# Latent attention, one head at a time, rewritten as pairs of heads with 64-row score products and a written-out order

## The chip, the core and the metric

The kernel runs on one NeuronCore of a Trainium2 chip. The metric is the device time of one execution in microseconds, as a median of several executions. Four engines do the arithmetic: TensorE (PE, matrix products; its weight loads are listed apart as PEld), VectorE (DVE), ScalarE (ACT) and GpSimd (POOL). SyncE (SP) issues most DMA transfers. Each engine works through its own instructions in order and waits on semaphores for the others. On-chip data lie in SBUF (128 partitions); matrix products are written to PSUM, eight banks of 512 float32 per partition.

## The reference

The program is two layers of a trunk over 1024 tokens of width 1024. Layer 0 uses differential attention, layer 1 latent attention; after each comes a gated MLP with a causal convolution of width 3. The change touches the latent attention alone:

```
proj = h @ w_in
c_q  = rms_norm(proj[..., :384], q_norm_g)
c_kv = rms_norm(proj[..., 384:640], kv_norm_g)
k_pe = apply_rope(proj[..., 640:], cos, sin)          # 32 wide, one for all heads
q  = (c_q @ w_uq).reshape(b, s, 16, 64 + 32)          # q_nope, q_pe (rotated)
kv = (c_kv @ w_ukv).reshape(b, s, 16, 64 + 64)        # k_nope, v
sc = (einsum(q_nope, k_nope) + einsum(q_pe, k_pe)) * 96 ** -0.5
p  = softmax(where(k // 64 <= q // 64, sc, min))      # causal in chunks of 64
o  = einsum(p, v).reshape(b, s, 1024) @ w_o
```

Sixteen heads; a query sees the keys of its own and all earlier chunks of 64.

## The kernel before

**Numbers in two parts.** To reach float32 accuracy with a fast product, every operand x is split into a high part (x rounded to the fast type) and a low part (x minus the high part). A product is three passes (`mm3`, L120 to L122): high by low, high by high, low by high. `hi` (L126, L128) makes the high part, on ScalarE unless another engine is named; `lo` (L131) makes the low part, on VectorE unless named.

**PSUM.** Three kinds of tiles share the eight banks: two "S" tiles of 128 x 1024 (two banks each), three "b" banks, one "u" bank.

**The stage.** `mla_input` works token tile by token tile (128 tokens, eight of them). It projects to the latents, normalizes them, transposes them, and makes the values, which go through DRAM (`v_d`) and come back head pair by head pair. Then come 64 steps, one for each head h and each p from 0 to 3. A step covers 256 queries, as two rows of 128 (j = 0, 1; row i = 2p + j has 128(i + 1) keys). Its parts are

- scores: one head's query tile holds 64 plain and 32 rotary rows, and 32 more so that the rotation becomes part of the product (128 rows in all); the key tile holds the matching 128 rows. Three full passes write an S tile in blocks of at most 512 keys. VectorE overwrites the masked corner (L2017), takes the row maximum (L2018); ScalarE takes the exponential with the row sum (L2019);
- VectorE inverts the sum (L2025), GpSimd scales the row (L150);
- PE transposes the weights in 128 x 128 blocks to a "b" bank (L264), ScalarE and VectorE split them (L128, L131);
- PE multiplies with the values, 64 high and 64 low columns side by side, in two passes (L2039, L2040) to the "u" bank; L2042 and L2043 add the halves; ScalarE issues the store of the result to `o_d` (L2045).

Beside the steps run the projections of the next head pair: for each head two halves of 512 tokens of the query (three latent blocks, nine passes each), and for each pair two halves of the keys (two blocks, six passes each). VectorE multiplies the query projection by the rotary table (L1720), ScalarE and mostly GpSimd split it; keys are split head by head in tiles of 64 rows.

**What sets the order.** In this stage the order of each engine's instructions is what the framework's scheduler makes of the program (`steps`, L293 on). In the differential attention of layer 0 it is written out by hand: a table with a line for each step names the parts in the order in which all four engines take them, and `manual_schedule` holds the scheduler to it. That attention's score products (L1884) are of 64 rows: the two halves of the array hold two different products, issued in turns.

After the attention comes the output projection, whose first half reads heads 0 to 7 alone, and the second MLP.

Of the kernel before, what the change touches and what calls it, by code (L numbers as in the profile page):

```python
# [44 lines left out]
class Ring:  # L45
# [5 lines left out]
    def __call__(self, shape, dt=F32):  # L51
        place = self.places[self.n % len(self.places)]
        self.n += 1
        return self.k.at(place, shape, dt)


class Trunk:
# [235 lines left out]
    def steps(self, attend, units, prepare, n, apart=False):  # L293


        steps = []
        for t in range(n + 2):
            now = before = None
            u = []
            if t < n:  # L300
                now = attend(t)
                steps.append(now)
                prepare(t)
                u = units(t)
                now.scores(0)
            if 0 < t <= n:
                before = steps[t - 1]
            alone = u[:-1] if apart else []
            if alone:
                u = u[-1:]  # L310
            self.run(alone or u, 2 if alone else 1)
            if before:
                before.turn()
            self.run(alone)
            if now:
                now.weigh(0)
                now.scores(1)
            self.run(u)
            if before:
                before.product()  # L320
            if now:
                now.weigh(1)
            if t >= 2:
                steps[t - 2].finish()
            yield

# [1213 lines left out]
    def mla_input(self, W, hts, turns, v_d, heads_of):  # L1540
# [24 lines left out]
        kp = [self.at(f"h{4 + half}", [MLA_ROPE, 512]) for half in range(2)]  # L1565
# [3 lines left out]
        def latents(i):  # L1569
# [5 lines left out]
            nat = nats([P, 672])  # L1575
# [4 lines left out]
            nc.scalar.copy(nat[:, 640:672], acc[:, 768:800])  # L1580
            return nat

        def turn(i, nat):
# [11 lines left out]
            for j in range(2):  # L1595
                nc.tensor.transpose(ps[:, j * P : (j + 1) * P], nat[:, (3 + j) * P : (4 + j) * P], self.ident)
            nc.tensor.transpose(ps[:MLA_ROPE, 256:384], nat[:, 640:672], self.ident)
# [3 lines left out]
            nc.scalar.copy(kp[half][:, s], ps[:MLA_ROPE, 256:384])  # L1601

        def values(i):
            half = i // 4
            s = slice((i % 4) * P, (i % 4 + 1) * P)
            vs = self.raw([P, D])
            for b, y in ((0, self.bank("u")), (512, self.bank())):
# [5 lines left out]
                nc.scalar.copy(vs[:, b : b + 512], y)  # L1613
            nc.sync.dma_start(v_d[:, :, i].rearrange("h p e -> p h e"), vs.rearrange("p (h e) -> p h e", e=P))

        def fetch_tab(half):
            late.tab = [self.at(place, [MLA_ROPE, 512]) for place in ("h12", "h13")]
            for x in range(2):
                nc.sync.dma_start(late.tab[x], a["rope_k"][:, x, half * 512 : (half + 1) * 512])

        def rotary(half):
            r = self.rope(rope, kp[half], *late.tab, MLA_ROPE // 2, MLA_ROPE)
            t = nats([MLA_ROPE, 2, 512], F32R)
            self.hi(t[:, 0, :], r[:MLA_ROPE])
            self.lo(t[:, 1, :], r[:MLA_ROPE], t[:, 0, :], nc.gpsimd)
            heads.rotary(half, t)
# [3 lines left out]
        for i in range(NT + 2):  # L1630
            if readies:
                readies.pop(0)()
            if i == NT - 2:
                heads.share(1, 0)
                heads.first(0, 2)
            if i == NT - 1:
                heads.first(4)
# [10 lines left out]
            if i == 4:  # L1648
                fetch_tab(0)
# [4 lines left out]
            if i == 5:  # L1654
                rotary(0)
                fetch_tab(1)
            if i == NT:
                rotary(1)
                heads.share(1, 1)
            if i >= 8:  # L1660
                heads.early()
        return heads

    SHARES = "SSSVVS"
    SHARED_AT = (3, 4, 10, 6)
    ROTARY = "SV"
    VALUES = "SSVSSSSS"
    WEIGHTS = "SVSSSSSS"
    QUERIES = "SSSVSSSSSSSSSSSSSSSSSSSSSSSSSSSS"
    QUERIES_LOW = "VPPVPPVPPPPPPPPPPPPPPPPPPPPPPPPP"  # L1670
# [665 lines left out]
```

## Time and profile before

| | |
|---|---|
| time, median of 3 runs | 2372.34 us (2372.22 to 2372.76) |
| the profiled execution | 2372.74 us, its span 2370.9 us |
| granted TensorE clock | 0.999 |
| PE busy | 2345.3 us, 99% of the span |
| PEld / DVE / ACT / POOL busy | 83% / 81% / 53% / 25% |
| differential attention | about 40 to 480 us |
| latents and values of layer 1 | about 1213 to 1300 us |
| steps of the latent attention | about 1290 to 1650 us |

Rows of the trace give the start of an instruction, how long it lasted, its engine, its line, what it writes and reads, and the shape. A PE pass lasts longer than the distance to the next pass's start, because passes overlap in the array; the distance from start to start is what a pass costs in a stream, and "busy" time overstates how well PE is used.

### The profile page before, as it was taken

The numbers are of one execution on the slowest core, as the hardware profiler recorded it, in microseconds if no ns is written. First come the engines' busy times: TensorE is split into PE (matmuls) and PEld (weight loads), VectorE is DVE, ScalarE is ACT, GpSimd is POOL, SyncE is SP. The second block draws the span as 40 slices with busy tenths as digits, with TensorE's granted clock in tenths as the row PEclk, the third lists the DMA queues.
The fourth block names the chain that finished last, engine by engine and source line by source line (L and its number), as shares of the span: only waits on it lengthen the run. The fifth ranks groups of instructions, "written<-read, shape, count | busy, mean of one in ns | idle before, by whom it ended". The sixth has DMA issues, their size and how long they took to land.

```text
span 2370.9 us, 32976 instructions
## 1 busy us (share of the span) xinstructions
PE 2345.3 (99%) x12146; PEld 1976.2 (83%) x12146; DVE 1919.9 (81%) x3170; ACT 1259.6 (53%) x2315; POOL 583.5 (25%) x465
## 2 busy tenths in 40 slices
PE   9999999999999999999999999999999999999998
PEld 7888888788888888888898889988888888888886
DVE  6777878858888888999865888886588888889997
ACT  5666666745444444354444777775454444443444
POOL 4545444323000000000133666673420000000001
PEclk9999999999999999999999999999999999999999
DMA  3111111332222222652221211133322222227502
GB/s 148 40 36 36 49 37 54 111 134 94 89 80 81 80 89 80 234 174 86 84 99 56 72 33 39 41 98 110 114 79 88 80 80 83 87 80 284 178 1 80
DMA packets 95667, 213.42 MB, mean 90 GB/s; under 512 B 8713, under 2 KB 33937, under 8 KB 95505
## 3 DMA queue, kind: packets, MB, share of 16 engines
q1 hardware_dynamic: 86304, 183.51, 23.5%
q10 hardware_dynamic: 9200, 27.80, 3.2%
q8 instruction: 96, 1.57, 0.3%
q14 instruction: 67, 0.54, 0.1%
HBM read 158.85 MB, written 52.43 MB: 89 GB/s over the span
## 4 chain that ended last, share of the span: by engine, by line
PE 91%; DVE 5%; DMA 1%; ACT 1%; issue 1%; POOL 0%; POOLq 0%; DVEq 0%; SPq 0%; ACTq 0%
PE S L122 14%; PE S L120 14%; PE S L121 14%; PE b L120 9%; PE b L122 8%; PE b L121 8%; PE u L120 5%; PE u L122 5%; PE u L121 4%; PE S L1884 3%; PE b L264 2%; PE u L2040 1%; PE b L1930 1%; PE u L2039 1%; DVE s L131 1%
## 5 line engine op out<-in xcount | busy, mean ns | idle before, releaser
L168 POOL TENSOR_TENSOR st<-st,mhalf 128x1 f32<-128x1 f32 x56 | 35.3, 632 | 1296.1 <-DVE st L165 1287.4
L120 PE MATMUL S<-s,u 128*128 128x512 f32 (+1 forms) x800 | 301.8, 377 | 0.2 <-ACT u L1110 0.2
L122 PE MATMUL S<-s,u 128*128 128x512 f32 (+1 forms) x800 | 301.2, 376 | 0.1
L121 PE MATMUL S<-s,u 128*128 128x512 f32 (+1 forms) x800 | 301.0, 376 | 0.0
L128 ACT CAST u<-h 128x512 fp32r<-128x512 f32 (+1 forms) x194 | 115.8, 619 | 267.1 <-DVE h L1031 262.8
L120 PE MATMUL b<-s,u 128*128 128x512 f32 x588 | 230.8, 393 | 1.1 <-DVE u L131 0.4
L122 PE MATMUL b<-s,u 128*128 128x512 f32 x588 | 229.1, 390 | 0.0
L121 PE MATMUL b<-s,u 128*128 128x512 f32 x588 | 229.0, 389 | 0.0
L1088 DVE SCALAR_TENSOR_TENSOR u<-u,conv,u 128x1023 f32<-128x1023 f32 (+1 forms) x176 | 225.1, 1279 | 0.8 <-ACT u L1084 0.7
L150 POOL TENSOR_TENSOR u<-u,st 128x512 f32<-128x512 f32 (+7 forms) x160 | 173.1, 1090 | 161.1 <-DVE st L2025 107.3
L128 ACT CAST s<-u 128x512 fp32r<-128x512 f32 (+3 forms) x229 | 144.2, 663 | 100.2 <-PE u L122 28.7
L128 ACT CAST u<-b 128x512 fp32r<-128x512 f32 (+1 forms) x256 | 134.9, 547 | 92.1 <-PE b L1930 57.7
L131 DVE TENSOR_TENSOR u<-b,u 128x512 fp32r<-128x512 f32 (+1 forms) x256 | 158.6, 631 | 23.9 <-ACT u L128 22.8
L120 PEld LDWEIGHTS S<-s,u 128*128 128x128 f32 x800 | 150.6, 188 | 27.9 <-ACT u L1110 0.5
L122 PEld LDWEIGHTS S<-s,u 128*128 128x128 f32 x800 | 150.6, 188 | 27.8 <-DVE u L131 0.3
L121 PEld LDWEIGHTS S<-s,u 128*128 128x128 f32 x800 | 150.6, 188 | 27.4
L120 PE MATMUL u<-s,s 128*128 128x512 f32 (+1 forms) x408 | 165.1, 405 | 1.1 <-DVE s L131 0.9
L122 PE MATMUL u<-s,s 128*128 128x512 f32 (+1 forms) x408 | 158.3, 388 | 0.0
L121 PE MATMUL u<-s,s 128*128 128x512 f32 (+1 forms) x408 | 157.6, 386 | 0.0
L131 DVE TENSOR_TENSOR s<-u,s 128x512 fp32r<-128x512 f32 (+2 forms) x205 | 140.8, 721 | 15.0 <-ACT s L128 14.7
L1091 ACT ACTIVATE u<-u 128x1024 f32<-128x1024 f32 x44 | 46.7, 1062 | 187.4 <-DVE u L1088 187.4
L131 DVE TENSOR_TENSOR u<-h,u 128x512 fp32r<-128x512 f32 x171 | 118.1, 691 | 32.4 <-ACT u L128 31.5
(294 smaller groups left out, 6389.6 us busy)
## 6 DMA issues: line engine op xcount, KB each, us to landing
u<-in_ffn_up SPq DMA_DIRECT2D x88, 512.0 KB, 3.9
g_d<-u ACTq DMA_DIRECT2D x44, 512.0 KB, 2.6
u<-in_ffn_down SPq DMA_DIRECT2D x66, 256.0 KB, 4.7
u<-g_d SPq DMA_DIRECT2D x62, 256.0 KB, 4.1
s<-in_da_wqkv SPq DMA_DIRECT2D x23, 512.0 KB, 3.3
x_d<-u SPq DMA_DIRECT2D x16, 512.0 KB, 2.6
s<-x_d SPq DMA_DIRECT2D x8, 1024.0 KB, 10.5
s<-g_d SPq DMA_DIRECT2D x18, 256.0 KB, 5.3
```

What stands on the lines that cost most here:

```text
L120: mm(out, lh, rl, start=first, stop=False, skip_group_check=onto)
L121: mm(out, lh, rh, start=False, stop=False, skip_group_check=onto)
L122: mm(out, ll, rh, start=False, stop=last, skip_group_check=onto)
L128: self.nc.scalar.copy(out, src)
L131: (eng or self.nc.vector).tensor_sub(out, src, hi.bitcast(F32))
L150: self.nc.gpsimd.tensor_mul(x, x, s.to_broadcast(list(x.shape)))
L168: nc.gpsimd.tensor_tensor(r, s, self.mhalf, ALU.pow)
L264: self.nc.tensor.transpose(ps[:, j * P : (j + 1) * P], probs[t][:, k : k + P], self.ident)
L1088: nc.vector.scalar_tensor_tensor(t[half][:, back:], u[half][:, : S - back], w, t[half][:, back:], ALU.mult, ALU.add)
L1091: nc.scalar.activation(t[0], t[0], AF.Silu)
L1884: nc.tensor.matmul(sc[c][:, b : b + m], q[rows, qp, qs], kt[rows, kp, :m], start=x == 0, stop=x == 2)
L1930: k.nc.tensor.transpose(ps[:, j * P : (j + 1) * P], self.e[t][0][:, c : c + P], k.ident)
```

## The change

**Heads in pairs.** A step is now one head pair and 256 queries: 32 steps. The 64 plain query rows of the two heads lie in one tile (head 0 in partitions 0 to 63, head 1 in 64 to 127), the keys likewise. Scores are products of 64 rows, the two heads' in turns (`scores` of the new `MlaStep`, L2080): five terms. Three are the plain part (low by high, high by low, high by high). Two are the rotary part: a tile `r` holds for each head 32 rows of the high and 32 of the low part of the rotated query, and the shared rotary key lies four times in partitions, so that `r` by the key's low and `r` by the key's high part make the rotary part.

**Shared query tiles.** The rotary queries of two head pairs (four heads x 32 rows) are projected together, every second pair (`r_parts`), and rotated with a shuffle, two products and a sum; the 64 plain rows of a pair are projected without the doubled rotary rows. Query scaling moves into the split (`q_parts`, L1745 for the low part).

**Mask as a product.** The corner is no longer overwritten: a sixth pair of 64-row products (L2083) adds a large negative number to it, out of a constant tile and 64 columns of ones.

**Where scores lie.** For p < 2 the two heads' scores share an S tile and one maximum instruction; for p > 1 each head has an S tile of its own, so that one row of scores takes both tiles.

**Values.** They are split before they go to DRAM and are read back ready (twice the bytes); the step that split them after reading is gone. The results' stores are now issued by SP, one in each step, out of two tiles in place of four.

**Order.** `mla_steps` reads a table of 32 lines; each names the parts (S scores, M maximum, E exponential, I inversion, C scaling, T transposes, H and L their split, A products with values, O and P the sum of halves; K, Q, R, W, V, O with numbers: projections and loads; a prime for each step back) in the order in which PE, DVE, ACT and POOL take them. The first four blocks of the output weights are split inside this order.

The PE queue before, in the middle of the stage, around the scores of one head (S tiles; b<-ident are transposes, u the products with values). Two rows of scores, each in three full passes for each block of keys, stand between transposes of the step before:

```order
L2040 MATMUL u_14576<-u_2552_14558,s_2412_13948 128x128
L264 MATMUL b_14617<-ident,u_2544_14520 128x128 x4
L264 MATMUL b_14625<-ident,u_2544_14520 128x128 x3
L120 MATMUL S_14713<-s_1919_11652,s_2434_14039 128x512
L121 MATMUL S_14713<-s_1919_11652,s_2434_14039 128x512
L122 MATMUL S_14713<-s_1919_11652,s_2434_14039 128x512
L120 MATMUL S_14713<-s_1919_11652,s_2434_14039 128x128
L121 MATMUL S_14713<-s_1919_11652,s_2434_14039 128x128
L122 MATMUL S_14713<-s_1919_11652,s_2434_14039 128x128
L120 MATMUL S_14769<-s_1919_11652,s_2434_14039 128x512
```

The PE queue of the change in the eleventh line of the table (p = 0, first row):

```order
L2146 MATMUL u_11986<-u_2187_13237,s_1967_11991 128x256
L2147 MATMUL u_11986<-u_2187_13237,s_1967_11991 128x256
L2080 MATMUL S_13287<-s_2086_12656,s_2087_12660 128x128 x4
L2080 MATMUL S_13287<-s_1917_11652,s_2051_12445 128x128 x4
L2080 MATMUL S_13287<-s_2086_12656,s_2087_12660 128x128 x2
L2083 MATMUL S_13287<-ones,h_1964_11982 128x64 x2
L2118 MATMUL b_13302<-ident,u_2161_13075 128x128
L2118 MATMUL b_13302<-ident,u_2166_13098 128x128 x2
L2146 MATMUL u_11986<-u_2193_13258,s_1967_11991 128x256
```

What moved: five pairs of 64-row passes and a mask pair now serve two heads, and full-height work (values, transposes) stands on both sides of them.

The VectorE queue before, around the same scores: a corner is overwritten (MEMSET) ahead of each maximum.

```order
L131 TENSOR_TENSOR u_2566_14622<-b_14617,u_2566_14622 128x512
L2017 MEMSET S_14713 64x64
L131 TENSOR_TENSOR u_2568_14629<-b_14625,u_2568_14629 128x384
L2018 TENSOR_REDUCE st_2588_14710<-S_14713 128x1
L2017 MEMSET S_14769 64x64
L2018 TENSOR_REDUCE st_2601_14766<-S_14769 128x1
```

The VectorE queue of the change at the end of the tenth line (p = 3, 1024 keys; S_13210 and S_13211 are the two heads') and the start of the eleventh:

```order
L1745 SCALAR_TENSOR_TENSOR s_2188_13241<-b_13175,s_2188_13241 128x512
L2090 TENSOR_REDUCE st_2190_13251<-S_13210 128x1
L2090 TENSOR_REDUCE st_2190_13251<-S_13211 128x1
L131 TENSOR_TENSOR u_2193_13258<-b_13246,u_2193_13258 128x512
L131 TENSOR_TENSOR h_2196_13285<-b_13254,h_2195_13284 128x384
L2090 TENSOR_REDUCE st_2199_13310<-S_13287 128x2
L2107 RECIPROCAL st_2191_13252<-st_2191_13252 128x2
```

What moved: no memset, two maxima of a wide row back to back, one maximum and one inversion for both heads where the row is short.

The diff, cut to its core:

```diff
+    def mla_steps(self, rows, attend, extra):
         steps = []
+        with self.tc.manual_schedule(engines={E.PE, E.DVE, E.Activation, E.Pool}):
+            for t, row in enumerate(rows):
+                for name in row.split():
+                    if name in extra:
+                        extra.pop(name)()
+                        continue
+                    step = t - name.count("'") + name.count("+")
+                    while len(steps) <= step:
+                        steps.append(attend(len(steps)))
+                    steps[step].parts.pop(name.strip("'+"))()
...
+    MLA = (
...
+        "S0 K30h C1a' Pb'''' H0a'' K30l C1b' L0a'' T1a'' M0a T2a'' H1a'' Q30 H2a'' M0b E0a L1a'' A0a''' E0b L2a'' A0b''' T0b'' Oa''' I0 S1 C0a Ob''' Pa''' H0b'' Pb''' Q30h L0b'' Q30l C0b T1b'' M1a T2b'' H1b'' T0a' A0a'' M1b E1a A1a'' A2a'' A0b'' L1b'' H2b''",
+        "S0 E1b' L2b''' T1a'' A1b''' M0 K31 Oa''' I1' C1a' H0a'' Pa''' H1a'' L0a'' S1 E0a L1a'' Q31 K31h M1 C1b' E0b K31l E1a I0 E1b T0b'' C0a Q31h I1",
...
+                vs = self.raw([P, D], F32R)
+                v = vs.rearrange("p (h a e) -> p h a e", a=2, e=64)
+                y = y.rearrange("p (h e) -> p h e", e=64)
+                self.hi(v[:, :, 0, :], y)
+                self.lo(v[:, :, 1, :], y, v[:, :, 0, :])
+                p = b // P
+                nc.sync.dma_start(v_d[p : p + 4, :, i].rearrange("h p e -> p h e"), vs.bitcast(F32).rearrange("p (h e) -> p h e", e=256))
...
+        v_ring, k_ring, q_ring, r_ring = self.ring("s13", "s4"), self.ring("s1", "s12"), self.ring("s11", "s5"), self.ring("s10", "s8")
+        t_ring = self.ring("h10", "h11", "h8")
...
-            P=self.ring("u12", "u6", "u7", "u8", "u9"), pT=self.ring("u0", "u1", "u10", "u11"), o=self.ring("h4", "h5", "h6", "h7"),
+            P=self.ring("u12", "u6", "u7", "u8", "u9", lambda: piece(0), lambda: piece(1)), pT=self.ring("u0", "u1", "u10", "u11", None), o=self.ring("h4", "h5"),
...
+        def project(p, off, n, latent, half):
             acc = self.bank()
+            for k in range(n):
+                wh, wl = (w[:, off + k * P : off + (k + 1) * P] for w in W[p])
+                self.mm3(acc, wh, wl, latent(0, half, k), latent(1, half, k), k == 0, k == n - 1)
+            return acc
+        def q_parts(p, half):
+            s, st = slice(half * 512, (half + 1) * 512), SimpleNamespace()
+            def products():
+                st.acc = project(p, 0, 3, cT.q, half)
+            def high():
+                if half == 0:
+                    pairs[p]["q"] = q_ring([P, 2, S], F32R)
+                nc.scalar.mul(pairs[p]["q"][:, 0, s], st.acc, MLA_SCALE)
+            def low():
+                q = pairs[p]["q"]
+                nc.vector.scalar_tensor_tensor(q[:, 1, s], st.acc, MLA_SCALE, q[:, 0, s].bitcast(F32), ALU.mult, ALU.subtract)
+            return {"": products, "h": high, "l": low}
...
+        def r_parts(p, half):
+            s, st, n = slice(half * 512, (half + 1) * 512), SimpleNamespace(), MLA_ROPE // 2
+            def products():
+                st.acc = project(p, 640, 3, cT.q, half)
+            def swap():
+                st.sw = t_ring([P, 512])
+                nc.vector.stream_shuffle(st.sw, st.acc, [i + n if i < n else i - n for i in range(32)])
+            def cosines():
+                st.r = t_ring([P, 512])
+                nc.vector.tensor_mul(st.r, st.acc, cosine[:, s])
+            def sines():
+                nc.gpsimd.tensor_mul(st.sw, st.sw, sine[half])
+            def add():
+                nc.gpsimd.tensor_add(st.r, st.r, st.sw)
+            def high(x):
+                if half == 0 and x == 0:
+                    t = r_ring([P, 2, S], F32R)
+                    for y in range(2):
+                        pairs[p + y]["r"] = t[:, y, :]
+                self.hi(pairs[p + x]["r"][:, s], st.r)
+            def low(x, c):
+                t = pairs[p + x]["r"][:, s]
+                src, dst = (slice(64 * c + 32 * y, 64 * c + 32 * y + 32) for y in (x, 1 - x))
+                self.lo(t[dst], st.r[src], t[src])
+            out = {"": products, "s": swap, "m": cosines, "p": sines, "a": add, "h": lambda: high(0), "g": lambda: high(1)}
...
+            R.mask = [self.at("h9", [P, P], F32R)]
+            nc.vector.tensor_scalar_mul(R.mask[0], self.ones.bitcast(F32), 0.0)
+            for c in range(2):
+                nc.vector.tensor_scalar_mul(R.mask[0][64 * c : 64 * c + 1, 0:64], self.ones[64 * c : 64 * c + 1, 0:64].bitcast(F32), NEG)
+            R.u = self.bank("u")
...
     def scores(self, j):
+        k, nc, hd = self.k, self.k.nc, self.hd
         i = 2 * self.p + j
         n = (i + 1) * P
+        q, kt, r, key = hd["q"], hd["k"], hd["r"], self.key[0]
         qs = slice(i * P, (i + 1) * P)
+        if self.one:
+            self.both[j] = k.big().rearrange("p (c n) -> p c n", c=2)[:, :, :n]
+            sc = [self.both[j][:, c, :] for c in range(2)]
+        else:
+            sc = [k.big()[:, :n] for _ in range(2)]
+        self.sc[j] = sc
         for b, m in blocks(n):
-            k.mm3(sc[:, b : b + m], q[:, 0, qs], q[:, 1, qs], kt[:, 0, b : b + m], kt[:, 1, b : b + m], True, True)
-        nc.vector.memset(sc[0:64, n - 64 : n], NEG)
+            s = slice(b, b + m)
+            terms = [(q[:, 1, qs], kt[:, 0, s]), (q[:, 0, qs], kt[:, 1, s]), (r[:, qs], key[:, 1, s]), (r[:, qs], key[:, 0, s]), (q[:, 0, qs], kt[:, 0, s])]
+            last = b + m == n
+            for x, (lhs, rhs) in enumerate(terms):
+                for c in range(2):
+                    rows = slice(64 * c, 64 * c + 64)
+                    nc.tensor.matmul(sc[c][:, s], lhs[rows], rhs[rows], start=x == 0, stop=x == 4 and not last, skip_group_check=last)
+        for c in range(2):
+            rows = slice(64 * c, 64 * c + 64)
+            nc.tensor.matmul(sc[c][:, n - 64 : n], self.R.mask[0][rows], k.ones[rows, 0:64], start=False, stop=True, skip_group_check=True)
+    def peak(self, j, c):
+        k = self.k
+        if j not in self.nm:
+            self.nm[j], self.l[j], self.e[j] = k.stat(2), k.stat(2), [None, None]
+        nm = self.nm[j] if c is None else self.nm[j][:, c : c + 1]
+        k.nc.vector.tensor_reduce(nm, self.both[j] if c is None else self.sc[j][c], axis=AX.X, op=ALU.max, negate=True)
+    def exp(self, j, c):
+        k, p = self.k, self.p
+        n = (2 * p + j + 1) * P
+        if p > 1:
+            e = self.R.P([P, S])[:, :n]
+        else:
+            x = j if p else 0
+            if x not in self.tile:
+                self.tile[x] = self.R.P([P, S])
+            off = c * 512 if p else j * 512 + c * 256
+            e = self.tile[x][:, off : off + n]
+        self.e[j][c] = e
+        k.nc.scalar.activation(e, self.sc[j][c], AF.Exp, bias=self.nm[j][:, c : c + 1], accum_out=self.l[j][:, c : c + 1])
...
+    def product(self, g, c):
+        k, nc, p = self.k, self.k.nc, self.p
+        if g == 0:
+            self.o[c] = self.R.u[:, c * 256 : c * 256 + 256]
+        o = self.o[c]
+        for kb, (ah, al), c0 in k.key_blocks(p, {x: self.pt.get((x, c), self.pt[g, c]) for x in range(p + 1)}):
+            if kb // 2 == g:
+                v = self.V[self.pair][:, kb, c].rearrange("p a e -> p (a e)")
+                nc.tensor.matmul(o[:, c0:], v, al, start=kb == 0, stop=False)
+                nc.tensor.matmul(o[:, c0:], v, ah, start=False, stop=kb == 2 * p + 1)
+    def copy(self, c):
+        if self.t is None:
+            self.t = self.R.o([64, 512])
+        self.k.nc.scalar.copy(self.t[:, c * 256 : c * 256 + 256], self.o[c][64:128])
+    def add(self, c):
+        t = self.t[:, c * 256 : c * 256 + 256]
+        self.k.nc.vector.tensor_add(t, t, self.o[c][0:64])
+        if not any(x in self.parts for x in ("Pa", "Pb")):
+            self.k.nc.sync.dma_start(self.dst, self.t.rearrange("e (c s) -> e c s", c=2))
...
```

365 lines of the change are left out of this document (158 added, 207 removed), and 30 rows, old and new, of the table MLA.

## The prediction

> **What bounds the kernel now.** I read first the busy times and the chain of waits on the page, then the busy time by stretches, then the instructions in order of time.
>
> ```profile
> PE 2345.3 (99%) x12146; PEld 1976.2 (83%) x12146; DVE 1919.9 (81%) x3170; ACT 1259.6 (53%) x2315; POOL 583.5 (25%) x465
> PE 91%; DVE 5%; DMA 1%; ACT 1%; issue 1%; POOL 0%; POOLq 0%; DVEq 0%; SPq 0%; ACTq 0%
> ```
>
> PE sets the time, and 91% of the chain is PE. So only two things count: what PE has to issue, and how long it finds nothing ready. In the next view each row is a stretch: its length, then the busy time of PE, PEld, DVE, ACT and POOL (instructions in brackets), the granted clock, the DMA's share and GB/s.
>
> ```profile
> 100.00:400.00 300.00, 300.00 (x1760) 245.21 (x1759) 237.53 (x436) 189.72 (x386) 149.77 (x107) 1.00 0.13 44
> ...
> 1300.00:1320.00 20.00, 17.66 (x95) 14.11 (x93) 18.04 (x33) 15.99 (x29) 14.20 (x10) 1.00 0.31 105
> 1320.00:1560.00 240.00, 239.30 (x1559) 215.50 (x1559) 199.08 (x488) 181.19 (x401) 157.73 (x128) 1.00 0.14 42
> 1560.00:1650.00 90.00, 87.76 (x560) 77.54 (x560) 69.42 (x154) 63.83 (x134) 52.09 (x40) 1.00 0.37 113
> 1290.00:1650.00 360.00, 354.72 (x2258) 315.20 (x2257) 293.65 (x692) 266.60 (x577) 229.34 (x180) 1.00 0.22 67
> ```
>
> In the stage that changes (1290 to 1650), PE is visibly idle for 360 - 354.72 = 5.3 us, 2.3 of them as the steps begin, 2.2 in the end, 0.7 in the 240 us between. The first row is the differential attention, with 64-row scores and a written-out order: no idle time at all in 300 us, with VectorE at 79%, ScalarE at 63%, GpSimd at 50%. It is the nearest thing to the changed stage that this trace has, and I take two prices from it. The clock is 1.00 throughout, so it is no term.
>
> **What a pass costs.** The distance from start to start is the price. Full height, in this stage:
>
> ```profile
> 1377.25 0.40 PE L121 MATMUL S<-s,s 128*128 128x512 f32 x1
> 1377.49 0.39 PE L122 MATMUL S<-s,s 128*128 128x512 f32 x1
> 1377.72 0.22 PE L120 MATMUL S<-s,s 128*128 128x128 f32 x1
> 1377.77 0.28 PE L121 MATMUL S<-s,s 128*128 128x128 f32 x1
> 1377.89 0.27 PE L122 MATMUL S<-s,s 128*128 128x128 f32 x1
> 1378.00 0.44 PE L120 MATMUL S<-s,s 128*128 128x512 f32 x1
> ...
> 1378.74 0.28 PE L120 MATMUL S<-s,s 128*128 128x256 f32 x1
> 1378.86 0.28 PE L121 MATMUL S<-s,s 128*128 128x256 f32 x1
> ```
>
> 512 columns cost 0.23 us, 256 cost 0.12, 128 cost 0.11 (the first one 0.05); 384 I put between, at 0.18. Half height, in the differential attention (x6 is three pairs, x12 six):
>
> ```profile
> 197.59 0.60 PE L585 MATMUL b<-ident,h 128*128 128x128 f32 x4
> 198.12 1.66 PE L1884 MATMUL S<-u,u 64*128 64x512 f32 x12
> 199.70 0.50 PE L120 MATMUL u<-s,s 128*128 128x512 f32 x1
> 200.04 0.40 PE L121 MATMUL u<-s,s 128*128 128x512 f32 x1
> ...
> 222.09 0.39 PE L122 MATMUL u<-s,s 128*128 128x512 f32 x1
> 222.41 0.97 PE L1884 MATMUL S<-u,u 64*128 64x512 f32 x6
> 223.31 0.55 PE L1930 MATMUL b<-ident,u 128*128 128x128 f32 x3
> 223.61 0.48 PE L1975 MATMUL b<-h,ones 128*128 128x512 f32 x1
> 223.93 0.40 PE L1976 MATMUL b<-h,ones 128*128 128x512 f32 x1
> ```
>
> Six pairs take 199.70 - 198.12 = 1.58 us, three take 223.31 - 222.41 = 0.90. So a further pair costs (1.58 - 0.90) / 3 = 0.23: two 64-row passes run at once for the price of one full pass. But 0.90 - 3 x 0.23 = 0.21 comes on top for each group. Also the pass before it is 0.32 long in place of 0.23 (222.09 to 222.41), and the first full pass behind it 0.34 (199.70 to 200.04). An excursion into half height and back to full passes thus costs 0.09 + 0.21 + 0.11 = 0.41. With three transposes behind it, they and the pass after them take 0.30 + 0.32 (223.31 to 223.93). Between full passes the same takes 0.24 + 0.32:
>
> ```profile
> 1440.85 0.49 PE L264 MATMUL b<-ident,u 128*128 128x128 f32 x3
> 1441.09 0.48 PE L120 MATMUL b<-s,u 128*128 128x512 f32 x1
> 1441.41 0.39 PE L121 MATMUL b<-s,u 128*128 128x512 f32 x1
> ```
>
> which is 3 x 0.11 + 0.23, so transposes beside full passes carry no charge. Behind half height they add 0.06, and the excursion makes 0.36. I take 0.38.
>
> The Trainium skill ("TensorEngine Tiling (Array Packing)", section Tiling Modes) says that changing the tiling mode drains TensorE, and its section Overview gives up to 2x for contractions of 64 rows or fewer. The trace agrees with both: the pair at 0.23 is the 2x, the 0.38 are the drains. By the second alone the sum below would lack its fourth term, which is the first rival.
>
> **PE's sum.** Four terms.
>
> Projections: before, 16 heads x 2 halves x 9 query passes and 8 pairs x 2 x 6 key passes, 384; after, 8 x 2 x (9 + 6) and 4 x 2 x 9 rotary ones, 312. 72 x 0.23 = -16.6.
>
> Scores: a head's eight rows have two blocks of 128, two of 256, two of 384, six of 512: one pass over all costs 2 x (0.11 + 0.12 + 0.18) + 6 x 0.23 = 2.20. Before, 16 heads x 3 x 2.20 = 105.6. After, 8 pairs x 5 terms x 2.20 = 88.0. -17.6.
>
> Mask: 64 extra pairs of 64 columns. The nearest row is the 128-column pass: 0.11, or 0.05 for the first one, whose successor's weights are not the limit. Half of 0.05 is the lower bound. 64 x 0.03 to 64 x 0.11 is 1.9 to 7.0; I take 7.0, since 128 columns already cost nearly what 256 do, so narrower passes stop getting cheaper. The Trainium skill ("TensorE: Matmul & The Clock Gate", section LDWEIGHTS) puts a weight load at the columns of the weights over 1.2 GHz whatever the rows; by it a mask pair would be an estimated 0.107 us, 6.8 in all.
>
> Excursions: 64 rows of scores, one for each j of 32 steps. Before, full passes join full passes and transposes without a charge. After, 64 x 0.38 = +24.3. If the mask's weight load falls into the drain, less; the 0.38 was read from three-pair and six-pair groups, which bounds it at 0.36 to 0.42, 23 to 27.
>
> Eight transposes of the latents grow from 32 to 128 columns: below 1 us, +0.6. Transposes (576) and value products (640) stay. Sum: -16.6 - 17.6 + 7.0 + 24.3 + 0.6 = **-2.3 us**. The 34 us that the counts promise are nearly eaten by drains and mask.
>
> **PE's idle time.** The waits behind it:
>
> ```profile
> PE S L120 <- ACT u L2019: 1.8, 3, 1.3
> PE b L264 <- DVE u L131: 1.1, 3, 0.6
> ```
>
> Eight such lines (5.1 us) make 13 waits; these are the longest. Each is longer than it looks by 0.16 us, since a pass lasts 0.39 and its successor is due after 0.23: 5.3 + 13 x 0.16 = 7.4 us, and gaps under 0.16 don't show at all. A written-out order had none in 300 us above, with less loaded helpers. In the new order the first steps lie among the value products, and the end among the output projection of heads 0 to 7, so both ragged places have cover. I take 10 us lost now and 2 then, **-8**; bounds 0 (nothing regained) and -12.
>
> **The other engines,** which only matter if they become late:
>
> ```profile
> L131 DVE TENSOR_TENSOR s<-b,s 64x512 fp32r<-64x512 f32 x30 | 20.6, 686 | 1.3 <-ACT s L128 0.8
> L1720 DVE TENSOR_TENSOR h<-b,u 128x512 f32<-128x512 f32 x30 | 20.6, 685 | 9.8 <-PE b L122 9.2
> L2018 DVE TENSOR_REDUCE st<-S 128x1 f32<-128x1024 f32 x16 | 19.6, 1223 | 1.2
> L2025 DVE RECIPROCAL st<-st 128x1 f32<-128x1 f32 x128 | 19.5, 152 | 7.9 <-ACT u L2019 7.6
> L2017 DVE MEMSET S<- 64x64 f32 x127 | 14.2, 112 | 10.4 <-PE S L122 8.9
> L249 DVE STREAM_SHUFFLE h<-h 32x512 f32<-32x512 f32 x1 | 0.7, 725 | 0.0
> L2019 ACT ACTIVATE u<-S,st 128x1024 f32<-128x1024 f32 x16 | 17.9, 1117 | 6.5 <-DVE st L2018 4.1 <-DVE st L2025 2.0
> L2019 ACT ACTIVATION_READ_ACCUMULATOR u<-S,st 128x1 f32 x128 | 25.3, 198 | 0.0
> L131 POOL TENSOR_TENSOR s<-h,s 128x512 fp32r<-128x512 f32 x28 | 36.2, 1294 | 1.0 <-ACT s L128 0.4
> L131 POOL TENSOR_TENSOR s<-u,s 128x1024 fp32r<-128x1024 f32 x9 | 21.6, 2395 | 2.5 <-ACT s L128 1.9 <-DVE st L2025 0.6
> s<-x_d SPq DMA_DIRECT2D x8, 1024.0 KB, 10.5
> ```
>
> VectorE loses the memsets (14), 32 table products (32 x 0.685 = 22), half the inversions (10), half the key lows (11). It gains 16 query lows (11), eight shuffles and eight products for the rotation (11), and 32 rotary lows of 32 rows. These cost a full 0.69 each, as the 32-row shuffle does (22). -13 in the stage, and 16 value lows of 0.69 (+11) ahead of it, where PE is the limit. So about 281 us of VectorE beside 350 of PE: 80%, what the written-out stage has. GpSimd loses the 36 us of query lows and gains eight pairs of rotary operations. ScalarE loses half its key and query splits. All this is hidden by PE; uncovered, nothing of it would exceed PE's time. The value loads double to 1 MB, at 10.5 us each as the x_d loads, and are issued many steps ahead: hidden. Stores and loads now share SP's queue: a weight load that waits for its buffer holds back a store behind it, and with two result tiles a store late by two steps (20 us) would stop ScalarE's copy and then PE. Since a buffer is freed by one GpSimd low of some 2.4 us, I charge nothing.
>
> **Sum.** The profiled execution took 2372.74, the median is 2372.34, 0.4 less. 2372.34 - 2.3 - 8 = **2362 us**.
>
> **Rivals.**
>
> 1. *The drains cost less* because the mask pair and the next transposes fill them, or the five terms stream better than three. Without the fourth term: 2372.3 - 16.6 - 17.6 + 1.9 + 0.6 - 8 = 2333. For it, the counts; against it, every 64-row group I looked at. 6%; half of the drains gone (2346) is the same case.
> 2. *No idle time comes back:* helpers as loaded as now stall PE as often. 2372.3 - 2.3 = 2370, no change that could be told. For it: VectorE is at 82% and ScalarE at 74% of this stage; in the model stage ScalarE has 63%. 19%.
> 3. *The score tiles become the bound: slower.* A wide row (p > 1, 32 of them) takes both S tiles at once; the next row of scores can start only after maximum and exponential of one or both heads. At 1024 keys: 1.22 + 1.22 for the maxima, then 1.12 + 0.20 for the second exponential, 3.8 us. In the tenth line PE has between its two rows three groups of transposes (1.3), a query projection (9 x 0.23 = 2.1) and two value products (1.0): 4.4. The margin is 0.6 us. If VectorE reaches the first maximum 1.1 us late in each of 32 rows, 0.5 is lost 32 times: 2370 + 16 = 2386. It decides from a mean lateness of 0.9 us on (0.3 x 32 = 10, which uses up the gain). For it: before, a row needed one tile and the other was free. Against: the table alternates wide rows with narrow ones, and hides this in line after line. 10%.
>
> My forecast has 65%. **Range:** the forecast's own 2354 to 2367; for 8 in 10, with the second rival and the near edge of the others, 2350 to 2375. A change of 0.2% (4.7 us) is about what can be told from none. Faster by more: 0.60 of the forecast's 0.65, the first rival, and a little of the second, where a few microseconds return: 0.70. Same: 0.05 and most of the second, 0.18. Slower: the third and some unlucky mixture, 0.12.
>
> **What would show it.** Right: 64-row groups of five pairs at 512 columns that take 5 x 0.23 + 0.11 + 0.2; about 64 of them with a 0.09 longer pass ahead; 312 projection passes; stage length 10 us less; PE idle under 2 us. Wrong: waits of S products on the exponential (third rival), of transposes on the lows (second), or groups without the 0.2 (first). A change in the MLP stages, whose code is the same, would be outside all of this.

## The result: slower by 16 us

The changed kernel takes 2388.77 us (median of 4; 2386.05 to 2389.40) where the kernel before took 2372.53 beside it (2372.22 to 2372.76): a ratio of 1.0066, 95% interval 1.0049 to 1.0084. The forecast was 2362, its range 2350 to 2375. Two single executions among the experiments, of 5191.73 us (experiment 4) and 3866.71 us (experiment 3), lie far above all others of their kernels and count in no time below.

First the busy times of the page, then PE, PEld, DVE, ACT and POOL in stretches of the profiled execution (span 2387.0 us):

```profile
PE 2342.4 (98%) x12586; PEld 1963.2 (82%) x12586; DVE 1912.1 (80%) x2976; ACT 1233.5 (52%) x2290; POOL 560.5 (23%) x447
```

```profile
1290.00:1320.00 30.00, 21.80 (x117) 16.67 (x117) 16.84 (x30) 13.77 (x35) 17.79 (x15) 0.83 0.51 168
1560.00:1660.00 100.00, 91.77 (x699) 79.96 (x696) 63.65 (x111) 63.03 (x141) 53.84 (x42) 0.97 0.26 78
1290.00:1650.00 360.00, 334.96 (x2600) 287.70 (x2598) 268.41 (x467) 234.96 (x541) 201.56 (x159) 0.98 0.21 67
```

Before, PE stood idle for 5.3 us in 1290 to 1650; now for 360 - 334.96 = 25, and the granted clock, which was 1.00 throughout, falls to 0.83 and 0.97 in two places. What PE waited for in this stage (total, times, longest):

```profile
PE S L2080 <- ACT u L2104: 14.4, 5, 8.2
PE u L2146 <- DVE h L2156: 4.7, 9, 0.6
PE b L2118 <- DVE s L131: 3.2, 3, 1.1
PE b L2118 <- DVE st L2107: 1.3, 1, 1.3
```

With four more lines (1.2 us) that makes 24.8 us in 23 waits, in place of 5.1 in 13. Two single waits of score products for exponentials are 13.8 of them. The first, as PE, ScalarE and SP show it:

```profile
1303.24 0.25 PE L2083 MATMUL S<-ones,h 64*128 64x64 f32 x2
1311.69 1.43 PE L2080 MATMUL S<-s,s 64*128 64x256 f32 x10 [8.20 <-ACT u L2104]
1312.92 0.25 PE L2083 MATMUL S<-ones,h 64*128 64x64 f32 x2
1313.11 0.79 PE L120 MATMUL b<-s,u 128*128 128x512 f32 x1
1313.70 0.63 PE L121 MATMUL b<-s,u 128*128 128x512 f32 x1
1314.12 0.63 PE L122 MATMUL b<-s,u 128*128 128x512 f32 x1
```

```profile
1308.13 1.67 ACT L128 CAST u<-u 128x640 fp32r<-128x640 f32 x2 [7.60 <-DMA u<-in_mla_w]
1310.18 0.69 ACT L2104 ACTIVATE u<-S,st 128x512 f32<-128x512 f32 x1
```

```profile
1299.74 2.29 SPq L1600 DMA_DIRECT2D v_d<-u  x2
1302.71 2.87 SPq L136 DMA_DIRECT2D u<-in_mla_w  x2
SPq L136 <- DMA v_d<-u: 2.6, 2, 2.0
```

Read from below: the raw weights of head pairs 1 and 2 are loaded into the same two tiles (`u14`, `u15`) from which the values are stored. So the loads are issued only when the last value stores have left, at 1302.7. The written order has the cast of these weights (`W1h` in the table's first line) ahead of the exponentials `E1a E1b`. ScalarE stands for 7.6 us, the exponentials come 8 us late, and the next row of scores with them. Behind it, 512-column passes come 0.42 apart for some microseconds instead of 0.23: the lower clock.

The second lies at the end, as PE, ScalarE, GpSimd and SP show it:

```profile
1595.96 2.50 PE L2080 MATMUL S<-s,s 64*128 64x512 f32 x10 [5.60 <-ACT u L2104]
1593.99 0.62 ACT L128 CAST h<-u 128x512 fp32r<-128x512 f32 x1 [5.40 <-DMA u<-o_d]
1595.02 0.79 ACT L2104 ACTIVATE u<-S,st 128x640 f32<-128x640 f32 x1
```

```profile
1586.93 4.70 POOL L131 TENSOR_TENSOR s<-u,s 128x1024 fp32r<-128x1024 f32 x2 [1.04 <-ACT s L128]
SPq L646 <- POOL s L131: 5.1, 2, 3.3
```

It is the same pair of tiles. The output projection's first operand load waits until GpSimd has split the output weights that lie there; its cast, which the scheduler put into ScalarE's queue between the lines of the table, stands ahead of an exponential.

### The profile page after: what moved, and what is told of

It is laid out like the page before. It is cut to its first block, busy times and chain, and to the rows that moved or that the text cites. A ratio compares the mean times of both kernels' runs of the same rounds, so it can differ in the third digit from the quotient of the medians.

```text
span 2387.0 us, 33667 instructions
## 1 busy us (share of the span) xinstructions
PE 2342.4 (98%) x12586; PEld 1963.2 (82%) x12586; DVE 1912.1 (80%) x2976; ACT 1233.5 (52%) x2290; POOL 560.5 (23%) x447
## 3 DMA queue, kind: packets, MB, share of 16 engines
q1 hardware_dynamic: 91136, 195.05, 24.8%
## 5 line engine op out<-in xcount | busy, mean ns | idle before, releaser
L128 ACT CAST u<-h 128x512 fp32r<-128x512 f32 x192 | 114.5, 619 | 264.7 <-DVE h L1013 262.6
L120 PE MATMUL b<-s,u 128*128 128x512 f32 x572 | 225.2, 394 | 0.4 <-DVE u L131 0.4
L121 PE MATMUL b<-s,u 128*128 128x512 f32 x572 | 223.3, 390 | 0.0
L122 PE MATMUL b<-s,u 128*128 128x512 f32 x572 | 223.1, 390 | 0.0
L128 ACT CAST u<-b 128x512 fp32r<-128x512 f32 (+1 forms) x232 | 122.6, 549 | 138.0 <-PE b L1965 57.7
L128 ACT CAST s<-u 128x512 fp32r<-128x512 f32 (+2 forms) x221 | 135.5, 650 | 104.5 <-PE u L122 29.6
L150 POOL TENSOR_TENSOR u<-u,st 128x128 f32<-128x128 f32 (+7 forms) x129 | 138.3, 1089 | 143.2 <-DVE st L2107 61.9
L131 DVE TENSOR_TENSOR u<-b,u 128x512 fp32r<-128x512 f32 (+1 forms) x232 | 143.0, 634 | 30.0 <-ACT u L128 29.9
L131 DVE TENSOR_TENSOR s<-u,s 128x512 fp32r<-128x512 f32 (+2 forms) x203 | 138.6, 717 | 15.6 <-ACT s L128 15.3
L131 DVE TENSOR_TENSOR u<-h,u 128x512 fp32r<-128x512 f32 x171 | 118.2, 691 | 32.8 <-ACT u L128 31.7
## 6 DMA issues: line engine op xcount, KB each, us to landing
s<-x_d SPq DMA_DIRECT2D x8, 1024.0 KB, 10.1
```

The lines of the kernel that those rows point to most:

```text
L120: mm(out, lh, rl, start=first, stop=False, skip_group_check=onto)
L121: mm(out, lh, rh, start=False, stop=False, skip_group_check=onto)
L122: mm(out, ll, rh, start=False, stop=last, skip_group_check=onto)
L128: self.nc.scalar.copy(out, src)
L131: (eng or self.nc.vector).tensor_sub(out, src, hi.bitcast(F32))
L150: self.nc.gpsimd.tensor_mul(x, x, s.to_broadcast(list(x.shape)))
```

## The experiments

**1. The two single waits.** Theory A: both come from the shared pair of raw tiles. Theory B: the two score tiles bound the rows (the prediction's third rival), and the loads only happen to be waited for at the same time.

The raw weights of pairs 1 and 2 in tiles that are free at that time:

```diff
-        raw = self.raw([P, w])
+        raw = self.at(place, [P, w]) if place else self.raw([P, w])
...
-            raws[p] = self.fetch(..., 640 if p % 2 else D)
+            raws[p] = self.fetch(..., 640 if p % 2 else D, {1: "u10", 2: "u11"}.get(p))
```

> The changed kernel with one edit: the raw weights of pairs 1 and 2 get tiles of their own (u10, u11) in place of the two tiles that they share with the value stores. Theory A (late loads ahead of hand-ordered work): the 8.2 us in which the score products of the second row wait for ScalarE's exponentials, which stand behind a cast that waits 7.6 us for these weights, goes, and with it the slower passes right after it (granted clock 0.95 in that 100 us): some 2.5 us. Time 2378, and the granted clock of 1300 to 1400 back at 1.00. Theory B (the two score tiles themselves bound the rows, the weights only happen to be waited for at the same time): the wait moves to the next exponential; time 2386 to 2389, and score products still wait for some 8 us in that place.

Measured: 2379.88 us (1.0032 of before, 1.0020 to 1.0045), 8.9 less than the change; 1.9 us less of a gain than expected. SP issues the two loads at 1284.65 and 1290.69, ahead of the last four value stores. The second of them, and the stretch of the first wait:

```profile
1290.69 0.35 SPq L136 DMA_DIRECT2D u<-in_mla_w  x1
1290.00:1320.00 30.00, 29.28 (x182) 22.77 (x181) 23.51 (x40) 19.12 (x46) 21.86 (x18) 1.00 0.52 176
```

PE is busy for 29.28 us in place of 21.80, and the clock is back at 1.00.

The output projection's operand loads in tiles of their own:

```diff
-        X = [None] * NT
+        X, raw = [None] * NT, self.ring("h12", "h13")
...
-                into = self.project(i, range(0, 4), W, o_d, os, self.raw)
+                into = self.project(i, range(0, 4), W, o_d, os, raw)
```

> The changed kernel with one other edit: the output projection's first operand loads get tiles of their own (h12, h13, free since the rotary is done) in place of the shared pair. Theory A: ScalarE's 5.4 us of waiting for such a load, between two exponentials, goes, and with it 5.6 us of idle TensorE and about 2 us of slower passes behind it (granted clock 0.97): 2381. Theory B: the score products wait for the next thing; 2387 to 2389.

Measured: 2383.16 (1.0046; 1.0031 to 1.0061), 5.6 less; 2 us less of a gain than expected.

Both:

> Both edits. Theory A: the two holes are apart (1303 and 1590 us) and add up: 10.7 + 7.6 = 18 us off 2388.8, so 2370.5, which is within 0.2% of the kernel before (2372.5): the change without the holes is worth about nothing, since its TensorE work is 4 us less and the small waits (some 15 us) stay about as many as before. If the order by rows had returned the idle time as forecast, it would be 2362. Theory B: 2384 or more.

Measured: 2374.26 (1.0009; 1.0000 to 1.0018), 14.5 less, the sum of the two. Theory A holds, and B falls: the scores' wait for exponentials shrinks from 14.4 us to 1.5. But what is left lies 3.8 us above the expected 2370.5, and is not the forecast of 2362. In 1290 to 1650:

```profile
1290.00:1650.00 360.00, 347.36 (x2675) 298.03 (x2675) 275.20 (x478) 239.36 (x550) 203.96 (x161) 1.00 0.23 72
PE u L2146 <- DVE h L2156: 4.7, 9, 0.6
PE b L2118 <- DVE s L131: 3.8, 4, 1.1
PE S L2080 <- ACT u L2104: 1.5, 4, 0.9
PE b L2118 <- DVE st L2107: 1.3, 1, 1.3
```

With three short lines, 12.3 us in 22 waits, still 7 more than before. The next experiments start from this kernel.

**2. What the 64-row products cost.** The five terms of a block over all 128 rows, three for one head and two for the other, so that the mode never changes. These are not the reference's scores. One mask pass of 128 rows stays, for the first head alone:

```diff
-                for c in range(2):
-                    rows = slice(64 * c, 64 * c + 64)
-                    nc.tensor.matmul(sc[c][:, s], lhs[rows], rhs[rows], start=x == 0, ...)
+                c = x % 2
+                nc.tensor.matmul(sc[c][:, s], lhs, rhs, start=x < 2, ...)
```

> The kernel with both edits, and its score products without the 64-row mode: each of the five terms of a block goes over all 128 rows in one pass, three of them to the first head's tile and two to the second's, and only the first head's block is masked. The scores are so not the reference's, and the time is that of the same number of columns without a change of mode. If the 64 excursions cost what the sum says (64 x 0.38 us), TensorE's work falls by 24 us, and the time by 15 to 24, since VectorE and ScalarE have 15 to 40 us of slack in that stage: 2347 to 2356. If the drains hide behind the weight loads or are a reading of modelled ends, the time stays at that of the kernel with both edits, 2370.

Measured: 2361.75 (0.9956; 0.9943 to 0.9970), 12.5 less: a gain, but a smaller one than the first case expected. The same place in three kernels, from the last pass before a group of ten pairs to the first transpose behind (the second one too in full rows): both tile edits, then full rows (lines shifted by one), then the kernel of the next experiment, without mask products (lines shifted back by one):

```profile
1392.62 0.27 PE L2118 MATMUL b<-ident,u 128*128 128x128 f32 x1
1392.82 2.58 PE L2080 MATMUL S<-s,s 64*128 64x512 f32 x20
1395.24 0.19 PE L2083 MATMUL S<-ones,h 64*128 64x64 f32 x2
1395.36 0.33 PE L2118 MATMUL b<-ident,s 128*128 128x128 f32 x1
```

```profile
1389.59 0.27 PE L2119 MATMUL b<-ident,u 128*128 128x128 f32 x1
1389.62 2.52 PE L2080 MATMUL S<-s,s 128*128 128x512 f32 x10
1391.97 0.19 PE L2084 MATMUL S<-ones,h 128*128 128x64 f32 x1
1392.00 0.30 PE L2119 MATMUL b<-ident,s 128*128 128x128 f32 x1
1392.14 0.27 PE L2119 MATMUL b<-ident,u 128*128 128x128 f32 x1
```

```profile
1393.58 0.27 PE L2117 MATMUL b<-ident,u 128*128 128x128 f32 x1
1393.78 2.58 PE L2080 MATMUL S<-s,s 64*128 64x512 f32 x20
1396.30 0.33 PE L2117 MATMUL b<-ident,s 128*128 128x128 f32 x1
```

2.74, 2.41 and 2.72 us. The 64-row group thus costs 0.33 more than full rows here (1395.36 - 1392.62 less 1392.00 - 1389.59), its mask pair 0.02. Between a projection and transposes, at 512 columns, it is 0.31 and 0.04. So the drains are real: 64 x 0.32 = 20 us of TensorE work. PE's waits grow as they go, to 17.2 us in 26, so the time falls by less than the work.

The 20 us are not the whole price, because the mask pass that full rows keep isn't free. Here it takes 0.03 itself, and the transpose behind it 0.14 (1392.00 to 1392.14) in place of 0.11; where a value product or a projection follows, that pass takes some 0.08 longer. The mean of 54 such places in this trace is 0.10. The 64-row group with its mask pair costs 0.30 more than full rows in the mean of the 51 rows of scores that no wait disturbs. I estimate from both that an excursion with its mask pair costs about 0.4 us more than full rows without a mask, 64 x 0.4 = 26 us; the sum had 24.3 + 7.0.

**3. The mask.** Filled by VectorE as before the change:

```diff
-            nc.tensor.matmul(sc[c][:, n - 64 : n], self.R.mask[0][rows], k.ones[rows, 0:64], ...)
...
+        k.nc.vector.memset(self.both[j][0:64, :, n - 64 : n] if c is None else self.sc[j][c][0:64, n - 64 : n], NEG)
```

> The kernel with both tile edits and the mask as it was before the change: a fill of 64 rows by VectorE ahead of each maximum in place of the product of 64 columns; in the rows with two short score blocks one fill covers both heads, so 96 fills of about 0.11 us instead of 64 pairs of products. By the prediction's sum the products cost TensorE 7.0 us (64 x 0.11), with bounds of 1.9 to 7.0. If all of this counts, the time falls from 2374.3 to about 2367, less what the fills put on the way from scores to maximum, 64 x 0.11 to 0.2 us, where TensorE waits for it; Rival: the way through maximum and exponential is as tight as TensorE there, and the time stays at 2373 to 2376.

Measured: 2377.06 (1.0020; 1.0012 to 1.0029): 2.8 more than with the products. Not even the rival's range holds it. The profiled execution, of 2375.12, was the shortest of the ten:

```profile
1290.00:1650.00 360.00, 342.61 (x2533) 286.10 (x2532) 287.83 (x567) 239.09 (x547) 203.56 (x161) 1.00 0.22 70
```

VectorE's busy time goes from 275.20 to 287.83 us, and PE's waits from 12.3 to 16.5. Beside 64-row scores a mask as a product is nearly free on TensorE and takes some 12 us off VectorE; this part of the change is worth having.

**4. A low part that waits for GpSimd.** The line `PE b L2118 <- DVE s L131` is in the main three waits of 1.1 us, 85 us apart. VectorE's rows ahead of the first, and GpSimd's:

```profile
1360.66 0.68 DVE L2090 TENSOR_REDUCE st<-S 128x2 f32<-128x512 f32 x1
1361.37 2.22 DVE L131 TENSOR_TENSOR s<-h,s 32x512 fp32r<-32x512 f32 x1
1359.31 3.75 POOL L150 TENSOR_TENSOR u<-u,st 128x1024 f32<-128x1024 f32 x2 [4.19 <-DVE st L2107]
```

A rotary low of 32 rows takes 2.22 us in place of 0.69, and behind three more such lows stands the key low that frees the bank. First, only the order on VectorE (and one place on ScalarE), in three places:

```diff
-... Q21 R21u E1a I0 R21g R21v C0a E1b R21w C0b T0b'' K21h I1",  "S0 R21x C1a' H0b''' K21l C1b' ...
+... Q21 K21h E1a I0 K21l R21u R21g R21v C0a E1b R21w C0b T0b'' I1",  "S0 R21x C1a' H0b''' C1b' ...
```

> The kernel with both tile edits (2374.3 us) and one more edit in the order: in the three places, 85 us apart, where TensorE's transposes wait 1.17 us for a PSUM bank, VectorE takes the low part of the key projection (which frees that bank) ahead of three of the four 32-row rotary lows, and ScalarE its high part one place earlier; nothing else is moved. Theory C (the 32-row lows, 0.69 us each and 2.22 us where one falls behind a GpSimd product, hold up what stands behind them on VectorE, and that ends on TensorE): three times 1.17 us go: 2370.8. Rival D (three banks are too few there, and the wait moves to the next transposes): 2374 to 2375. The 2.22 us low itself is expected to stay in the trace, since the GpSimd product beside it has not moved.

Measured: 2371.37 (0.9996; 0.9987 to 1.0005), 2.9 less: theory C. One part of the expectation missed: the long low is gone as well. Moved behind the key low, it starts at 1362.71, at the end of the GpSimd product, and takes 0.68.

Second, the order as it was, but the scaling beside that low on ScalarE:

```diff
-        self.k.scale(self.e[j][c], self.l[j][:, c : c + 1], "P")
+        self.k.scale(self.e[j][c], self.l[j][:, c : c + 1], "A" if self.pair in (1, 3, 5) and (self.p, j, c) == (3, 1, 1) else "P")
```

> The kernel with both tile edits (2374.3 us, its rotary low of 2.22 us in three places), with one scaling of 128x1024 in each of these three places moved from GpSimd to ScalarE; the order stands. Theory G (a 32-row low, whose operands both lie in SBUF, can't run while a GpSimd product runs, and waits for its end): without that product beside it the low takes 0.69 us, and the transposes behind it wait some 0.2 us instead of 1.17, if ScalarE, which gets 1.05 us more, does not hold them up instead: 2371. Rival H (the low is slow there for another reason, its source or its place in the queue): it stays at 2.2 us, and the time at 2374.

Measured: 2371.14 (0.9995; 0.9986 to 1.0004), 3.1 less.

```profile
1361.45 0.68 DVE L131 TENSOR_TENSOR s<-h,s 32x512 fp32r<-32x512 f32 x1
1359.39 1.90 POOL L150 TENSOR_TENSOR u<-u,st 128x1024 f32<-128x1024 f32 x1 [4.14 <-DVE st L2107]
```

The same low, in the same place of VectorE's queue, without a GpSimd product beside it: 0.68. Theory G. The mean of the lows in the stage falls from 932 to 767 ns:

```profile
L131 DVE TENSOR_TENSOR s<-h,s 32x512 fp32r<-32x512 f32 x28 | 26.1, 932 | 0.9
L131 DVE TENSOR_TENSOR s<-h,s 32x512 fp32r<-32x512 f32 x28 | 21.5, 767 | 0.9
```

**5. The rest of the small waits.** The largest group is `PE u L2146 <- DVE h L2156`. One bank holds both heads' outputs; the program orders every read of it against every product into it, whichever head's columns they touch:

```profile
1371.51 0.27 PE L2147 MATMUL u<-u,s 128*128 128x128 f32 x1
1371.88 0.41 DVE L2156 TENSOR_TENSOR h<-h,u 64x256 f32<-64x256 f32 x1 [0.74 <-ACT u L128]
1372.34 0.39 PE L2146 MATMUL u<-h,s 128*128 128x256 f32 x1 [0.56 <-DVE h L2156]
```

VectorE's sum for one head (its copy is done at 1371.01) starts only when the other head's products have ended, and the next product waits for it. The profile puts VectorE's 0.74 us down to a cast that the sum doesn't read; but in the seven longest of these waits the sum starts 0.03 to 0.10 us behind the end of the other head's last product, so I read that as its releaser. The last kernel starts from the one with the key low first and moves some 95 more entries of the table by a few places, in 24 of its 32 lines; one of them (the ninth) before and after:

```diff
-        "S0 E1b' L2b''' T0a'' M0 T0b'' H3b''' S1 H0b'' I1' L3b''' E0a C1a' L0b'' K30 Oa''' M1 E0b C1b' A0b''' I0 E1a Pa''' A1b''' A2b''' C0a H0a'' A3b''' E1b L0a'' C0b T0a' Ob''' I1",
+        "S0 E1b' L2b''' M0 T0b'' H3b''' S1 H0b'' I1' L3b''' T0a'' Oa''' M1 E0b E0a C1a' C1b' A0b''' I0 E1a Pa''' L0b'' K30 C0a A1b''' A2b''' H0a'' A3b''' E1b L0a'' C0b T0a' Ob''' I1",
```

Between `Pa'''` and the next products (`A1b'''`) a key projection now stands, and covers the sum.

> Both tile edits, the key low first, and further moves in the table of rows: some 110 of its 1455 entries stand a few places earlier or later, none is added or dropped, and what each computes is the same. They go against the waits that the trace of the kernel with the key low first still shows in this stage, each of 0.15 to 1.4 us and most of them three times, 85 us apart: products that wait while ScalarE or VectorE reads the one PSUM bank that both heads' outputs share (5.3 us in 11 places), scores that wait for exponentials (1.5 us), transposes that wait for a bank (2 us). Theory E (these waits are a matter of order alone): with the durations of that trace laid out in the new order, 10 to 12 us of them are gone: 2371.4 falls to 2360, some 0.5% under the kernel before. Rival F (VectorE, ScalarE and GpSimd, each 50 to 80% busy here, pass the delay on, and the waits turn up elsewhere): 2368 to 2372.

Measured: 2361.24 (2359.67 to 2362.05): 0.9952 of before, 0.9938 to 0.9966. Theory E. It takes less time than the kernel before and the change. All of PE's waits in the stage, and the stage's busy times:

```profile
PE u L2146 <- DVE h L2156: 0.9, 3, 0.3
PE b L2118 <- DVE s L131: 0.8, 1, 0.8
PE b L120 <- DVE u L131: 0.4, 1, 0.4
PE S L2080 <- ACT u L2104: 0.2, 1, 0.2
PE b L2118 <- DVE h L131: 0.2, 1, 0.2
1290.00:1650.00 360.00, 356.66 (x2743) 307.37 (x2742) 278.43 (x488) 243.41 (x557) 204.73 (x163) 1.00 0.25 80
```

2.5 us in 7 waits. GpSimd's products still catch rotary lows here, and the longest wait that is left (0.8 us, at 1313) stands behind one of them, of 2.58 us at 1309.79; behind the others TensorE no longer waits for a low.

## Why the prediction was wrong

**The step that failed is PE's idle time:** "I take 10 us lost now and 2 then, -8; bounds 0 (nothing regained) and -12." A loss was excluded, and a loss it was: the listed waits went from 5.1 to 24.8 us. Three things stood behind the step.

1. *The comparison with the differential attention.* I took a written-out order that loses nothing in 300 us as the sign of what a written-out order does. It showed that such an order can lose nothing, not that this one does. Without the two long waits (2374.26) this table loses 12.3 us, where the scheduler's order lost 5.1; with some 100 entries moved it loses 2.5 (2361.24). For the kernel without the two long waits, the second rival, "no idle time comes back", with 2370, was the nearest case.
2. *The two ends of the stage.* "The first steps lie among the value products, and the end among the output projection of heads 0 to 7, so both ragged places have cover." In just these two places the work that was to be cover shares its buffers with the steps' loads, and a load that is late for its buffer stops ScalarE, which all steps need. I had the danger in view ("a weight load that waits for its buffer") and looked for it behind SP, at the stores, not at the engine that reads the load; "a buffer is freed by one GpSimd low of some 2.4 us, I charge nothing" left out that value stores hold these buffers too. 14.5 us by experiment 1, the lower clock included.
3. *The rotary lows "cost a full 0.69 each" and are hidden.* Their mean in the stage was 932 ns; three of them at 2.22 us cost about 3 us of TensorE (experiment 4).

**TensorE's work** was right in sign and too high in one term, the mask: 0.02 to 0.04 a pair, some 2 us, near the lower bound of 1.9 and not at 7.0. Behind 64-row scores a narrow pass does not cost what a 128-column pass costs; in full rows, at 0.10, it nearly does. The excursions held: the 0.31 to 0.33 of experiment 2 are counted from a kernel that pays for its mask pass, and 0.4 less a mask pair of 0.03 is about the 0.38 that I took. With 2 us for the mask the sum is -16.6 - 17.6 + 2 + 24.3 + 0.6, about -7. The traces agree: the profiled spans of the last kernel and of the one before differ by 2360.3 - 2370.9 = -10.6, of which the listed waits are 2.5 - 5.1 = -2.6, and 6 waits fewer at 0.16 each are 1.0. That leaves -7 for the work.

**The third rival** was right in what waits (scores for exponentials) and wrong in why: with the loads out of the way, this wait is 1.5 us. That its 2386 lies near the measured 2388.77 is luck. **The first rival** was wrong: without the mode changes 12.5 us go, so they were being paid.

Of the signs I had named, the price of a group nearly held (five pairs at 512 columns and the mask pair took 1.39 us where I had 1.46), and waits of transposes on the lows did show the second rival; PE idle under 2 us and a stage 10 us shorter did not come. That 2361 came out in the end, close to the forecast, is the worth of the change once its order and its buffers are repaired. It is not what the change as made did, and that it lies so close is luck: the work gave more than the -2.3 of the sum, the idle time less than its -8.

## What to carry to other kernels

When an order is written out by hand, follow every DMA that an entry reads from back to the last reader of its buffer; an entry whose load may be late belongs behind everything that does not need it, or its load into a buffer of its own. A stage that loses nothing shows what an order can do; for another stage, add up the wait at each place from durations of rows, including which engines shut each other out. Where a few waits come back with a fixed period, small moves pay: nine entries gave 2.9 us here and some 95 more another 10.1, where the saved arithmetic is worth 7.

## What the hardware showed beside this

**VectorE and GpSimd shut each other out** when VectorE has both operands in SBUF. In the traces of four kernels, each rotary low that began well inside a GpSimd product ended 0.53 to 0.55 us after that product's end (above: 1361.37 + 2.22 = 1363.59, and 1359.31 + 3.75 = 1363.06), and a 128x128 scaling that began during a low took 0.83 to 0.90 us in place of 0.40. The key lows before the change read one operand from PSUM (64 rows, 0.686 us mean): 18 of the 30 began inside a GpSimd instruction, and each of these took 0.66 to 0.69 us all the same. The Trainium skill ("SBUF — State Buffer", section Who interferes with whom) states that a VectorE instruction with two SBUF inputs contends with a GpSimd instruction that reads SBUF, that the port pair that they share is an exclusive lock, and that the order of issue decides which of them blocks; the rows agree.

**After a wait of 8 us TensorE runs slower for a while.** In the trace of the change the last pass ahead of the first long wait ends at 1303.49. The granted clock is 1.00 from 1303.6 to 1305.7 and 0.50 from 1305.9 on; passes of 512 columns came 0.42 apart from 1313.7 on, and 0.23 again from 1316.2 on. Over the 30 us from 1290 the clock was 0.83. Behind waits of up to 2.4 us (the kernel with full rows) the clock of the stretch stayed at 1.00. The Trainium skill ("TensorE: Matmul & The Clock Gate", section Part 1) tells of a clock that is halved after an idle window of some 3.4 us. The trace agrees on the halving, behind 5.6 us and 8.2; here the clock fell some 2.3 us after the last pass had ended, sooner than that figure. So a long wait costs more than its length, here some 2 us beside the 8.2. Beside the same passes in experiment 1, the score group behind the wait took 0.6 longer (1.42 against 0.81) and the pass after it 0.26 (0.59 against 0.33); the next five took 0.2 longer each, and one more 0.12.
